# Chunk recurrence of an RWKV-7 mixer: two heads per full-array product, and the preparation of two pairs of heads side by side

## Chip, cores and metric

The kernel runs on one core of a Trainium2 chip, in one launch. The metric is the device time of that core in microseconds (us); lower is better. Several runs are timed and their median counts.

## What is computed

One residual block on x of 1024 frames x 1024 features: a SwiGLU layer, a mixer, a second SwiGLU layer, each behind an RMS norm whose shift, scale and gate come from a conditioning vector. Half of the mixer is chunked attention (8 heads of 64), half is the RWKV-7 recurrence (8 heads of 64), which is what the change touches:

```python
def step(state, inp):
    r_t, w_t, k_t, v_t, kk_t, b_t = inp
    sa = jnp.einsum('bhvk,bhk->bhv', state, -kk_t)
    state = (state * w_t[:, :, None, :] + sa[..., None] * b_t[:, :, None, :]
             + v_t[..., None] * k_t[:, :, None, :])
    y_t = jnp.einsum('bhvk,bhk->bhv', state, r_t)
    return state, y_t
...
_, ys = lax.scan(step, state0, seq_first)
```

Everything is computed in float32; the large products are split into three products of float32r parts.

## The kernel before

The 1024 frames are two halves, hf = 0 and 1, of 512 frames (8 chunks of 64). The order of all instructions is written at build time by a planner: tasks are Python generators that yield what they wait for, `drive` (L285) runs the one whose wait ends first on a modelled clock, and where nothing else is due it takes the next block of the **main products** (`mm`, tiles of 128x512 float32r, fed by weights that SyncE loads as `wst`, ScalarE rounds to `whi` and VectorE completes as `wlo`). So the products of attention and recurrence stand between main products on TensorE. The main products in their order are: first layer of half 0 (f1A), projection of half 0 (pA), first layer of half 1 (f1B), output projection of half 0 (oA), projection of half 1 (pB), second layer of half 0 (f2A), output projection of half 1 (oB), second layer of half 1 (f2B). Recurrence and attention of half 0 run beside f1B, those of half 1 beside f2A. Each engine executes its instructions in the planned order and waits for semaphores where data is late.

The recurrence works on four pairs of heads (p = 0 to 3) in each half, two pairs to a group:

- `rwkv1` (L1203) prepares one pair: masked products GR and GA (banks `gb`), transposed keys BKn (banks `bt`), decays `gC`. `RA` holds r and a, `BKB` the keys. In `rwkv` (L1542) the second pair's preparation starts when the first one's has ended.
- `inverse` (L1344) inverts the triangular 32x32 blocks of a group on VectorE, through DRAM (`nd`), and loads them into `TT`.
- `rwkv2` (L1386) is the recurrence of one pair. It completes `TT` by 32x32 products (`qb`, `ub`), then takes 8 chunks in turn. A chunk has three steps: `px` = GA·UV, copied to X; `pu` = TT·X, copied into UV; `pz` = BKn·UV, from which the next state Z and the next UV are made. Each step is one product per head, 64 columns wide: px and pz have 128 rows and 64 columns of the array (128*64), pu 64 and 64 (64*64), and the two heads take two tiles of the array. After the loop, `yb` reads all UV and Z at once. That is 3 steps x 8 chunks x 4 pairs x 2 halves = 192 steps.

UV is a tile of its own per head (16 loads `UV<-vs` of 128 KB each in all), filled with the values before `TT` is waited for. The pools `set0` and `set1` have 16 slots of 128x512 each.

Of the kernel before, what the change touches and what calls it, by code (L numbers as in the profile page):

```python
# [16 lines left out]
P = 128  # L17
# [228 lines left out]
class Builder:  # L246
# [113 lines left out]
    def setup(self):  # L360
# [3 lines left out]
        self.sets = [self.pool("set0", 16), self.pool("set1", 16)]  # L364
# [54 lines left out]
    def setup2(self):  # L419
# [107 lines left out]
    def ada_first(self, v):  # L527
# [5 lines left out]
        def load(i, v=v):  # L533
            q, kb = steps[i]
            n = 2 if (v, q) in ADA_PE else 2 if v or kb in (0, 3) else 3
            w[v, i] = self.tile(self.sets[1], "n1", 16, "wa", [P, 2, 256], reads=n)
            nc.sync.dma_start(w[v, i], self.a["w_ada"][v, :, 2 * kb : 2 * kb + 2, q * 256 : q * 256 + 256])
# [63 lines left out]
    def ada(self, vs):  # L601
# [101 lines left out]
    def norm_first(self):  # L703
# [18 lines left out]
        for q in range(4):  # L722
# [16 lines left out]
    def norm(self, key, hf, j, src=None):  # L739
        nc = self.nc  # L740
        s = self.sets[hf]
# [12 lines left out]
        nh, nl, vs = [], [], []  # L754
# [6 lines left out]
        def low(d):  # L761
            nc.vector.scalar_tensor_tensor(nl[d], vs[d], scale(d)[1], nh[d].bitcast(F32), op0=OP.add, op1=OP.subtract)

        def step(d, x):
            yield x, rstd, "th", f"n{hf}", lambda: 0.0 if len(self.mains) < 2 else self.clock.at["vector"]
            sc, sh = scale(d)
# [3 lines left out]
            nh.append(self.tile(s, f"n{hf}", 16, "nh", dt=F32R))  # L770
            nl.append(self.tile(s, f"n{hf}", 16, "nl", dt=F32R))
# [373 lines left out]
    def tb(self, hf, name, shape=None):  # L1145
        return self.tile(self.sets[hf], f"n{hf}", 16, name, shape)
# [56 lines left out]
    def rwkv1(self, hf, p):  # L1203
# [70 lines left out]
        BKB = self.sm("BKB", [P, NC, 3, C], 1)  # L1274
# [5 lines left out]
        nc.scalar.activation(BKB[:, :, 2], BKB[:, :, 0], AF.Copy)  # L1280
# [8 lines left out]
        GR, GA, BKn = [], [], []  # L1289
        for h in range(2):  # L1290
            yield f"n{hf}"
            GR.append(self.tb(hf, "GR", [P, NC, C]))
            yield f"n{hf}"
            GA.append(self.tb(hf, "GA", [P, NC, C]))
        half = [slice(0, 64), slice(64, 128)]
        for c4 in range(2):
            yield BKB, RA, self.two
            gb = [self.bank("gb", 2) for h in range(2)]
            for i in range(4):
                c = 4 * c4 + i  # L1300
                for h, s in enumerate(half):
                    self.mm(
                        gb[h][:, i * P : i * P + P],
                        BKB[s, c, h : h + 2].rearrange("p k t -> p (k t)"),
                        RA[s, c].rearrange("p k t -> p (k t)"), side=2,
                    )
            for h in range(2):
                g4 = gb[h].rearrange("p (c k t) -> p c k t", c=4, k=2)
                for k, o in ((1, GA[h]), (0, GR[h])):
# [7 lines left out]
        for c in range(NC):  # L1317
            for h, s in enumerate(half):
                self.tp_(
                    bt[h][:, c * C : c * C + C],  # L1320
                    BKB[s, c, h : h + 2].rearrange("p k t -> p (k t)"),
                    self.ident[s, s], side=2,
                )
        for h in range(2):
            yield f"n{hf}"
            BKn.append(self.tb(hf, "BKn", [P, NC, C]))
            nc.scalar.activation(BKn[h], c3(bt[h]), AF.Copy)
# [8 lines left out]
        for h in range(2):  # L1336
            yield GA[h]
            for b in range(2):
                q = h * 64 + b * 32
                w = (4 * i + 2 * h + b) * 8  # L1340
                nc.sync.dma_start(nd[w : w + 8].rearrange("c s t -> s c t"), GA[h][q : q + 32, :, b * 32 : b * 32 + 32])
        return dict(p=p, RA=RA, GR=GR, GA=GA, BKn=BKn, bon=bon, gC=gC)

    def inverse(self, hf, st):  # L1344
# [26 lines left out]
        for i in range(2):  # L1371
# [3 lines left out]
            nc.gpsimd.memset(TT, 0.0)  # L1375
        yield ud
        for i in range(2):
            for h in range(2):
                for b in range(2):
# [4 lines left out]
                    )  # L1384

    def rwkv2(self, hf, st):  # L1386
        nc = self.nc
        p, RA, GR, GA, BKn, TT = (st[k] for k in ("p", "RA", "GR", "GA", "BKn", "TT"))
# [12 lines left out]
        U1 = self.tr("U1", [P, NC, 32])  # L1401
        for h in range(2):
            r0 = slice(h * 64, h * 64 + 32)
            nc.vector.transpose(U1[r0], TT[r0, :, 0:32])
        yield U1, "b"
        qb = self.bank("qb", 2)
        for c in range(NC):
            for h in range(2):
                r0 = slice(h * 64, h * 64 + 32)
                r1 = slice(h * 64 + 32, h * 64 + 64)  # L1410
                self.mm(
                    qb[r1, c * 32 : c * 32 + 32], GA[h][r0, c, 32:64], U1[r0, c],
                    tile_position=(h * 64, h * 64 + 32), side=2,
                )
        yield qb
        for h in range(2):
            r1 = slice(h * 64 + 32, h * 64 + 64)
            nc.scalar.activation(U1[r1], qb[r1, 0:256].rearrange("p (c t) -> p c t", c=NC), AF.Copy)
        yield U1, TT, "b"
        ub = self.bank("ub", 2)  # L1420
        for c in range(NC):
            for h in range(2):
# [3 lines left out]
                    ub[r0, c * 32 : c * 32 + 32], U1[r1, c], TT[r1, c, 32:64],  # L1426
# [8 lines left out]
        nc.scalar.activation(GA[0][0:64], RA[0:64, :, 1], AF.Copy)  # L1435
        nc.gpsimd.tensor_copy(GA[1][64:128], RA[64:128, :, 1])

        Z = self.tr("Z", [P, NC, C])
        nc.vector.tensor_copy(Z[:, 0], self.Zc[p])
        for c in range(NC):  # L1440
            yield *GA, *UV, "b"
            px = self.bank("px")
            for h in range(2):
                self.mm(px[h * 64 : h * 64 + 64, 0:C], GA[h][:, c], UV[h][:, c], skip_group_check=True)
            X = self.sm("X", [P, C], 4, reads=2)
            nc.vector.tensor_copy(X, px[:, 0:C])
            zg = self.sm("zg", [P, C], 3, reads=3 if c + 1 < NC else 1)
# [276 lines left out]
```

## Time and profile before

| | us |
|---|---|
| median of 3 runs | 2178.19 (2175.65 to 2180.26) |
| profiled execution, time | 2181.82 |
| profiled execution, span of the trace | 2180.1 |
| PE (TensorE matmul) busy | 2136.9 |
| DVE (VectorE) busy | 1463.8 |
| ACT (ScalarE) busy | 897.1 |
| POOL (GpSimd) busy | 128.4 |

Engine shares are averages over stages with different limits. Matmul durations in the trace are modelled and overlap: what one costs is read from the distance between the starts of instructions. One product written in float32 is two instructions in the trace (so px counts 256 for 64 steps of two heads), one in float32r a single one. In the notation 128*64 128x64, the first pair is the rows and columns of the array in use, the second the partitions and elements that stream in. All 11568 matmul instructions of the program are in the trace.

### The profile page before, as it was taken

To read this page: it belongs to the slowest core of one execution; us is meant where nothing else is said; L and a number is where in the kernel's file an instruction comes from. 1 tells how busy PE (TensorE), PEld (TensorE's weight loads), DVE (VectorE), ACT (ScalarE), POOL (GpSimd) and SP (SyncE) were. 2 spreads that over 40 slices of the span, in tenths; PEclk is the share of its full clock that TensorE was granted. 3 is DMA by queue.
4 is the path that set the end of the run, shared out by engine and by line. 5 is a ranking of instruction groups with operands and counts; after the bars stand their busy time and mean duration, and the time that the engine had idled before them with its cause. 6 is when DMAs were issued, how large, how long until landed. Compare 5 with 4: busy or idle time off the path is not lost.

```text
span 2180.1 us, 32870 instructions
## 1 busy us (share of the span) xinstructions
PE 2136.9 (98%) x11568; PEld 1718.1 (79%) x11568; DVE 1463.8 (67%) x3090; ACT 897.1 (41%) x1712; POOL 128.4 (6%) x166
## 2 busy tenths in 40 slices
PE   6999999999999999999999999999999999999999
PEld 4788887888778868877888777867786888888887
DVE  6977777744578877877864567878787664444444
ACT  4332224445555344333555555435442343222322
POOL 1000000011300000000020300001000000000000
PEclk9999999999999999999999999999999999999999
DMA  7766655435764424334645745324432554433333
GB/s 236 243 201 210 202 161 173 132 116 160 234 189 132 121 71 125 105 94 123 215 153 163 217 146 159 110 81 128 120 106 64 184 167 141 136 97 98 96 93 102
DMA packets 230853, 316.31 MB, mean 145 GB/s; under 512 B 61976, under 2 KB 97824, under 8 KB 230688
## 3 DMA queue, kind: packets, MB, share of 16 engines
q1 hardware_dynamic: 230688, 314.22, 47.7%
q8 instruction: 91, 1.49, 0.3%
q14 instruction: 74, 0.61, 0.1%
HBM read 279.52 MB, written 34.61 MB: 144 GB/s over the span
## 4 chain that ended last, share of the span: by engine, by line
PE 86%; DMA 6%; DVE 4%; ACT 2%; issue 2%; SPq 1%; POOL 0%; DVEq 0%; ACTq 0%; POOLq 0%
PE mm L512 72%; PE mmb L512 3%; PE yp L512 1%; DMA vd<-av 1%; PE tr L516 1%; PE S L512 1%; DMA kd<-kT 1%; SPq L172 1%; PE cs L516 1%; DVE wlo L172 1%; PE gb L512 1%; PE pu L512 1%; DMA wst<-in_ffn_w 1%; PE px L512 1%; PE pz L512 1%
## 5 line engine op out<-in xcount | busy, mean ns | idle before, releaser
L172 ACT ACTIVATE whi<-wst 128x512 fp32r<-128x512 f32 (+2 forms) x692 | 423.2, 613 | 840.2 <-PE mm L512 692.1
L172 DVE TENSOR_TENSOR wlo<-wst,whi 128x512 fp32r<-128x512 f32 (+2 forms) x692 | 462.3, 671 | 341.2 <-ACT whi L172 328.0
L512 PE MATMUL mm<-nh,whi 128*128 128x512 f32 x1520 | 616.7, 406 | 0.0
L512 PE MATMUL mm<-nl,whi 128*128 128x512 f32 x1520 | 594.2, 391 | 4.3 <-DVE nl L172 4.3
L512 PE MATMUL mm<-nh,wlo 128*128 128x512 f32 x1520 | 594.8, 391 | 0.0
L512 PEld LDWEIGHTS mm<-nh,wlo 128*128 128x128 f32 x1520 | 286.0, 188 | 61.4
L512 PEld LDWEIGHTS mm<-nh,whi 128*128 128x128 f32 x1520 | 286.7, 189 | 56.4 <-issue 1.9
L512 PEld LDWEIGHTS mm<-nl,whi 128*128 128x128 f32 x1520 | 286.8, 189 | 56.1 <-DVE nl L172 5.7
L512 PE MATMUL mm<-ah,whi 128*128 128x512 f32 x670 | 273.3, 408 | 2.1 <-ACT ah L172 1.2
L512 PE MATMUL mm<-al,whi 128*128 128x512 f32 x670 | 262.4, 392 | 1.5 <-DVE al L172 1.5
L512 PE MATMUL mm<-ah,wlo 128*128 128x512 f32 x670 | 262.5, 392 | 1.1 <-DVE wlo L172 1.1
L172 DVE SCALAR_TENSOR_TENSOR h<-mm,g,h 128x512 f32<-128x512 f32 x183 | 135.9, 746 | 89.6 <-PE mm L512 88.9
L512 PEld LDWEIGHTS mm<-ah,whi 128*128 128x128 f32 x670 | 126.5, 189 | 30.1 <-ACT ah L172 2.1
L512 PEld LDWEIGHTS mm<-ah,wlo 128*128 128x128 f32 x670 | 126.3, 188 | 28.6 <-DVE wlo L172 1.5
L512 PEld LDWEIGHTS mm<-al,whi 128*128 128x128 f32 x670 | 126.6, 189 | 24.8 <-DVE al L172 2.4
L172 ACT ACTIVATE E<-E,st 128x640 f32<-128x640 f32 (+4 forms) x128 | 85.8, 688 | 32.4 <-DVE st L172 32.0
L172 DVE SCALAR_TENSOR_TENSOR acc<-wa,silc,acc 128x512 f32<-128x512 f32 (+1 forms) x120 | 83.5, 705 | 0.6
L172 DVE TENSOR_TENSOR sw<-sw,mm 128x512 f32<-128x512 f32 x85 | 58.4, 687 | 35.7 <-PE mm L512 32.3
L172 ACT ACTIVATE pt<-tr 128x256 fp32r<-128x256 f32 x144 | 49.4, 344 | 65.8 <-PE tr L516 60.4
L512 PE MATMUL mm<-whi,nh 128*128 128x512 f32 x184 | 73.8, 401 | 0.0
L512 PE MATMUL mm<-wlo,nh 128*128 128x512 f32 x184 | 71.8, 390 | 0.0
L512 PE MATMUL mm<-whi,nl 128*128 128x512 f32 x184 | 71.7, 390 | 0.0
(247 smaller groups left out, 2631.3 us busy)
## 6 DMA issues: line engine op xcount, KB each, us to landing
wst<-in_ffn_w SPq DMA_DIRECT2D x468, 256.0 KB, 2.8
wa<-in_w_ada SPq DMA_DIRECT2D x144, 256.0 KB, 4.0
wst<-in_w_v SPq DMA_DIRECT2D x64, 256.0 KB, 2.9
wst<-in_ffn_w SPq DMA_DIRECT2D x64, 192.0 KB, 2.4
wst<-in_w_t SPq DMA_DIRECT2D x40, 256.0 KB, 4.1
wst<-in_w_out SPq DMA_DIRECT2D x32, 256.0 KB, 3.0
kd<-kT SPq DMA_DIRECT2D x48, 128.0 KB, 3.9
bias<-in_bias SPq DMA_DIRECT2D x16, 320.0 KB, 4.2
```

What stands on the lines that cost most here:

```text
L172: return f(*args, **kw)
L512: self.nc.tensor.matmul(out, lhsT, rhs, start=start, stop=stop, **kw)
L516: self.nc.tensor.transpose(out, in_, ident)
```

## The change

- The three steps of a chunk become one product each of 128 rows and 128 columns, with the two heads side by side in the streamed 128 columns or, in pu, on the diagonal of a 128x128 tile X (`Xd`, cleared once). pu takes two neighbouring chunks of TT as its 128 columns and uses 64 of the rows that come out.
- GA, BKn and UV hold both heads in one tile. UV is now a part of RA (its second and third column blocks), so the mask part of RA is first copied to GA, by ScalarE for both heads; the values are loaded after that, in one load of 256 KB per pair.
- X is copied half by VectorE, half by ScalarE; UV is copied by ScalarE for both heads; Z is copied from UV by ScalarE, where VectorE computed it a second time.
- TT's first blocks of the second head are loaded once more to partitions 0 to 31 (`T1`), and both heads' `qb` products read rows 0 to 31 of the array.
- The preparations of the two pairs of a group are tasks of their own: the second starts when RA of the first is written (`RA` in `done`), and in the second group each follows the recurrence of a pair of the first.
- The pools `set0` and `set1` become 8 slots of 128x512 and 4 of twice that; the ring `tr` has 8 slots for 10. The low parts `nl`, `ml` and some weights `wa` go in twos into the large slots. `mx` moves from the ring `th` to `tr`.

The core of the diff:

```diff
-        self.sets = [self.pool("set0", 16), self.pool("set1", 16)]
+        self.sets = [self.pool("set0", 8), self.pool("set1", 8)]
...
+        self.Xd = [cp.tile([P, P], F32, name=f"Xd{i}") for i in range(4)]
+        for x in self.Xd:
+            nc.gpsimd.memset(x, 0.0)
...
+    def slot(self, hf, name, shape=None, dt=F32, reads=None):
+        return self.tile(self.sets[hf], f"n{hf}", 8, name, shape, dt, reads)
+    def slots(self, hf, name, shape, dt=F32, reads=None):
+        return self.tile(self.sets[hf], f"d{hf}", 4, name, shape, dt, reads)
...
-        return self.tile(self.sp, "tr", 10, name, shape, dt, reads)
+        return self.tile(self.sp, "tr", 8, name, shape, dt, reads)
...
-        RA = self.sm("RA", [P, NC, 2, C], 2)
+        RA = self.sm("RA", [P, NC, 3, C], 2)
...
+        self.done.add(f"RA{hf}{p}")
...
-        nc.scalar.activation(BKB[:, :, 2], BKB[:, :, 0], AF.Copy)
...
+        yield f"d{hf}"
+        GA = self.slots(hf, "GA", [P, NC, 2, C])
...
+            yield "tr"
+            st[i]["T1"] = self.tr("T1", [32, NC, 32], reads=1)
...
-        UV = []
-        vsr = self.vs[hf].rearrange("(c t) f -> t c f", t=C)
-        for h in range(2):
-            yield "tr"
-            UV.append(self.tr("UV", [P, NC, C]))
-            o = slice(64 - h * 64, 128 - h * 64)
-            nc.vector.tensor_copy(UV[h][h * 64 : h * 64 + 64, 0], self.Zc[p][h * 64 : h * 64 + 64])
-            nc.sync.dma_start(UV[h][o], vsr[:, :, p * P + h * C : p * P + h * C + C])
-        yield TT, "tr"
-        U1 = self.tr("U1", [P, NC, 32])
-        for h in range(2):
-            r0 = slice(h * 64, h * 64 + 32)
-            nc.vector.transpose(U1[r0], TT[r0, :, 0:32])
+        heads = [slice(0, 64), slice(64, 128)]
+        hv = lambda t: t.rearrange("p h v -> p (h v)")
+        yield TT, T1, "tr"
+        U1 = self.tr("U1", [P, 2, NC, 32])
+        nc.vector.transpose(U1[0:32, 0], TT[0:32, :, 0:32])
+        nc.vector.transpose(U1[0:32, 1], T1)
...
-                    qb[r1, c * 32 : c * 32 + 32], GA[h][r0, c, 32:64], U1[r0, c],
-                    tile_position=(h * 64, h * 64 + 32), side=2,
+                    qb[r1, c * 32 : c * 32 + 32], GA[0:32, c, h, 32:64], U1[0:32, h, c],
+                    tile_position=(0, h * 64 + 32), side=2,
...
-        nc.scalar.activation(GA[0][0:64], RA[0:64, :, 1], AF.Copy)
-        nc.gpsimd.tensor_copy(GA[1][64:128], RA[64:128, :, 1])
+        for h, s in enumerate(heads):
+            nc.scalar.activation(GA[0:64, :, h], RA[s, :, 1], AF.Copy)
+        yield GA
+        UV = RA[:, :, 1:3]
+        for h, s in enumerate(heads):
+            nc.vector.tensor_copy(UV[0:64, 0, h], self.Zc[p][s])
+        vsr = self.vs[hf].rearrange("(c t) f -> t c f", t=C)
+        nc.sync.dma_start(
+            UV[64:128].rearrange("p c h v -> p c (h v)"), vsr[:, :, cs]
+        )
         Z = self.tr("Z", [P, NC, C])
         nc.vector.tensor_copy(Z[:, 0], self.Zc[p])
+        Tf = TT.rearrange("p c t -> p (c t)")
         for c in range(NC):
-            yield *GA, *UV, "b"
-            px = self.bank("px")
-            for h in range(2):
-                self.mm(px[h * 64 : h * 64 + 64, 0:C], GA[h][:, c], UV[h][:, c], skip_group_check=True)
-            X = self.sm("X", [P, C], 4, reads=2)
-            nc.vector.tensor_copy(X, px[:, 0:C])
-            zg = self.sm("zg", [P, C], 3, reads=3 if c + 1 < NC else 1)
+            yield GA, UV, "b"
+            px = self.bank("px", 2)
+            self.mm(px[:, 0:P], hv(GA[:, c]), hv(UV[:, c]))
+            X = self.Xd[p % 2 * 2 + c % 2]
+            nc.vector.tensor_copy(X[0:64, 0:64], px[0:64, 0:64])
+            nc.scalar.activation(X[64:128, 64:128], px[64:128, 64:128], AF.Copy)
+            zg = self.sm("zg", [P, C], 3, reads=2)
             gc = st["gC"][:, c : c + 1]
             nc.vector.tensor_scalar(zg, Z[:, c], gc, None, OP.mult)
             yield X, TT, "b"
-            pu = self.bank("pu", 2)[:, 0:C]
-            for h in range(2):
-                s = slice(h * 64, h * 64 + 64)
-                self.mm(pu[s], TT[s, c], X[s])
-            nc.scalar.activation(UV[0][0:64, c], pu[0:64], AF.Copy)
-            nc.vector.tensor_copy(UV[1][64:128, c], pu[64:128])
-            yield *UV, "b"
-            pz = self.bank("pz", 3 if c + 1 < NC else 1)[:, 0:C]
-            for h in range(2):
-                s = slice(h * 64, h * 64 + 64)
-                self.mm(pz[s], BKn[h][:, c], UV[h][:, c])
-            for h in range(2 if c + 1 < NC else 0):
-                s = slice(h * 64, h * 64 + 64)
-                nc.vector.scalar_tensor_tensor(UV[h][s, c + 1], pz[s], gc[s], zg[s], op0=OP.mult, op1=OP.add)
-            zn = Z[:, c + 1] if c + 1 < NC else self.Zc[p]
-            nc.vector.scalar_tensor_tensor(zn, pz, gc, zg, op0=OP.mult, op1=OP.add)
-        self.free(TT, *BKn)
+            pu = self.bank("pu", 1)
+            t = min(c, NC - 2) * C
+            self.mm(pu[:, 0:P], Tf[:, t : t + P], X)
+            nc.scalar.activation(hv(UV[0:64, c]), pu[heads[c == NC - 1], 0:P], AF.Copy)
+            yield BKn, UV, "b"
+            pz = self.bank("pz", 2)
+            self.mm(pz[:, 0:P], hv(BKn[:, c]), hv(UV[:, c]))
+            for h, s in enumerate(heads):
+                zn = UV[0:64, c + 1, h] if c + 1 < NC else self.Zc[p][s]
+                nc.vector.scalar_tensor_tensor(zn, pz[s, h * 64 : h * 64 + 64], gc[s], zg[s], op0=OP.mult, op1=OP.add)
+            for h, s in enumerate(heads if c + 1 < NC else []):
+                nc.scalar.activation(Z[s, c + 1], UV[0:64, c + 1, h], AF.Copy)
+        self.free(TT, BKn)
...
-    def rwkv(self, hf, g, st):
-        if g == 0:
-            yield from self.rwkv_prep(hf)
-        for i in range(2):
-            st.append((yield from self.rwkv1(hf, 2 * g + i)))
-        yield from self.inverse(hf, st)
     def spawn_rwkv(self, name, hf, after):
-        v = f"{name}v"
+        v, up = f"{name}v", f"{name}p"
         self.spawn(v, self.values(hf), 3, [f"v{hf}"])
+        self.spawn(up, self.rwkv_prep(hf), 2, after)
+        before = [up, up]
         for g in range(2):
-            st = []
-            self.spawn(f"{name}{g}", self.rwkv(hf, g, st), 2, after)
-            after = []
+            st = {}
+            pre = [f"{name}{g}p{i}" for i in range(2)]
+            for i in range(2):
+                x = [before[i]] + [f"RA{hf}{2 * g}"] * i
+                self.spawn(pre[i], self.late(lambda st=st, p=2 * g + i: self.rwkv1(hf, p, st)), 2, x)
+            self.spawn(f"{name}{g}", self.late(lambda st=st: self.inverse(hf, st)), 2, pre)
+            before = []
             for i in range(2):
                 n = f"{name}{g}_{i}"
                 self.spawn(n, self.late(lambda st=st, i=i: self.rwkv2(hf, st[i])), 2 + i, [f"{name}{g}", v])
-                after.append(n)
-        self.spawn(name, self.end_rwkv(), 2, after)
+                before.append(n)
+        self.spawn(name, self.end_rwkv(), 2, before)
```

On TensorE, in the recurrence of the first two pairs of half 0, before (`yp` is a product of attention, `nh`, `nl` are the parts of the normed input):

```order
L512 MATMUL px_7680<-UV_7434,GA_6332 64x64
L512 MATMUL px_7680<-UV_7437,GA_6334 64x64
L512 MATMUL mm_7592<-nh_3569,whi_7451 128x512
L512 MATMUL mm_7592<-nl_3570,whi_7451 128x512
L512 MATMUL mm_7592<-nh_3569,wlo_7452 128x512
L512 MATMUL pu_7695<-X_7683,TT_7396 64x64 x2
L512 MATMUL pu_7700<-X_7668,TT_7398 64x64 x2
L512 MATMUL yp_7705<-pt_7634,V_7216 128x256 x2
L516 MATMUL tr_7708<-ident,E_7477 128x128
L516 MATMUL tr_7708<-ident,E_7507 128x128
```

and in the changed kernel (UV bears the name of its tile, RA; X that of its tile, Xd):

```order
L523 MATMUL pu_7622<-Xd_2991,TT_7279 128x128
L523 MATMUL pu_7626<-Xd_2990,TT_7276 128x128
L523 MATMUL mm_7561<-nh_3535,whi_7421 128x512
L523 MATMUL mm_7561<-nl_3491,whi_7421 128x512
L523 MATMUL mm_7561<-nh_3535,wlo_7422 128x512
L523 MATMUL pz_7634<-RA_6225,BKn_6474 128x128
L523 MATMUL pz_7640<-RA_6496,BKn_6694 128x128
L523 MATMUL mm_7561<-nh_3550,whi_7421 128x512
L523 MATMUL mm_7561<-nl_3547,whi_7421 128x512
L523 MATMUL mm_7561<-nh_3550,wlo_7422 128x512
L523 MATMUL px_7652<-RA_6225,GA_6349 128x128
```

Two products of 64x64 (two rows, or one with x2) have become one of 128x128. Main products stand between the steps as before.

On SyncE, where the recurrence of the first group begins, before (`nd_1` is the inverse on its way back, `vs` holds the values):

```order
L172 DMA nd_1_3089<-BKB_6866 64x1024
L172 DMA wst_7415<-in_ffn_w 128x512
L172 DMA TT_7396<-nd_1_3089 32x8x32 x4
L172 DMA TT_7398<-nd_1_3089 32x8x32 x4
L172 DMA UV_7434<-vs_3080 64x8x64
L172 DMA UV_7437<-vs_3080 64x8x64
L172 DMA UV_7440<-vs_3080 64x8x64
L172 DMA UV_7443<-vs_3080 64x8x64
L172 DMA wst_7455<-in_ffn_w 128x512
```

and in the changed kernel:

```order
L172 DMA TT_7276<-nd_1_3030 32x8x32 x4
L172 DMA T_1675_7278<-nd_1_3030 32x8x32
L172 DMA TT_7279<-nd_1_3030 32x8x32 x4
L172 DMA T_1677_7281<-nd_1_3030 32x8x32
L172 DMA wst_7323<-in_ffn_w 128x512
L172 DMA wst_7342<-in_ffn_w 128x512
L172 DMA wst_7369<-in_ffn_w 128x512
L172 DMA wst_7463<-in_ffn_w 128x512
L172 DMA RA_6225<-vs_3021 64x8x128
L172 DMA kd_7523<-kT_3025 64x512 x2
L172 DMA qd_7526<-qT_3023 64x512 x2
L172 DMA RA_6496<-vs_3021 64x8x128
```

The values go to RA instead of UV, in one load per pair instead of two, and behind four loads of weights where they stood right behind those of TT.

## Rows read from the trace of the kernel before

**Rows 1.** Page, part 1: busy us, share of the span, instructions.

```profile
PE 2136.9 (98%) x11568; PEld 1718.1 (79%) x11568; DVE 1463.8 (67%) x3090; ACT 897.1 (41%) x1712; POOL 128.4 (6%) x166
```

**Rows 2.** Page, part 4: the chain that ended last, by engine.

```profile
PE 86%; DMA 6%; DVE 4%; ACT 2%; issue 2%; SPq 1%; POOL 0%; DVEq 0%; ACTq 0%; POOLq 0%
```

**Rows 3.** PE timeline at 763 us: start, duration, instruction; one step between main products.

```profile
762.94 0.39 PE L512 MATMUL mm<-nl,whi 128*128 128x512 f32 x1
763.17 0.40 PE L512 MATMUL mm<-nh,wlo 128*128 128x512 f32 x1
763.49 0.34 PE L512 MATMUL px<-UV,GA 128*64 128x64 f32 x4
...
764.09 0.39 PE L512 MATMUL mm<-nl,whi 128*128 128x512 f32 x1
```

**Rows 4.** PE timeline at 803 us: two steps of one tiling.

```profile
802.93 0.39 PE L512 MATMUL mm<-nh,wlo 128*128 128x512 f32 x1
803.25 0.34 PE L512 MATMUL pz<-UV,BKn 128*64 128x64 f32 x4
803.41 0.29 PE L512 MATMUL px<-UV,GA 128*64 128x64 f32 x4
...
803.97 0.39 PE L512 MATMUL mm<-nl,whi 128*128 128x512 f32 x1
```

**Rows 5.** PE timeline at 974 us: two steps of different tilings.

```profile
974.08 0.39 PE L512 MATMUL mm<-ah,wlo 128*128 128x512 f32 x1
974.40 0.33 PE L512 MATMUL pu<-X,TT 64*64 64x64 f32 x4
974.66 0.34 PE L512 MATMUL px<-UV,GA 128*64 128x64 f32 x4
...
975.26 0.39 PE L512 MATMUL mm<-al,whi 128*128 128x512 f32 x1
```

**Rows 6.** PE timeline at 1010 us: four full-array float32 products of 128 columns.

```profile
1010.61 0.39 PE L512 MATMUL mm<-nh,wlo 128*128 128x512 f32 x1
1010.84 1.05 PE L512 MATMUL gate<-wu,sgd 128*128 128x128 f32 x8
...
1011.96 0.40 PE L512 MATMUL mm<-nl,whi 128*128 128x512 f32 x1
```

**Rows 7.** Groups by form: instructions, count, busy us, mean ns, idle before.

```profile
L512 PE MATMUL px<-UV,GA 128*64 128x64 f32 x256 | 21.3, 242 | 0.2 <-DVE Z L172 0.2
```

**Rows 8.** The same groups: the 32x32 products that complete TT.

```profile
L512 PE MATMUL qb<-U,GA 32*32 32x32 f32 x256 | 5.5, 192 | 0.0
```

**Rows 9.** ACT groups at the start of a recurrence.

```profile
L172 ACT ACTIVATE TT<-ub 32x256 f32<-32x256 f32 x16 | 6.0, 372 | 3.3 <-PE ub L512 3.2
L172 ACT ACTIVATE GA<-RA 64x512 f32<-64x512 f32 x8 | 5.1, 633 | 0.2
```

**Rows 10.** DMA issues: count, KB each, median us from issue to landing.

```profile
UV<-vs SPq DMA_DIRECT2D x16, 128.0 KB, 3.1
vn<-vs SPq DMA_DIRECT2D x8, 256.0 KB, 4.7
```

**Rows 11.** VectorE and ScalarE groups of a chunk.

```profile
L172 DVE COPY UV<-pu 64x64 f32<-64x64 f32 x64 | 14.1, 227 | 19.9 <-ACT UV L172 18.5
L172 DVE SCALAR_TENSOR_TENSOR Z<-pz,gC,zg 128x64 f32<-128x64 f32 x56 | 15.9, 284 | 1.6
L172 ACT ACTIVATE UV<-pu 64x64 f32<-64x64 f32 x64 | 13.5, 217 | 88.6 <-PE pu L512 81.2 <-DVE D L172 5.3 <-DVE zg L172 1.6
```

**Rows 12.** Windows, 500 to 1700 us: busy us of PE, PEld, DVE, ACT, POOL.

```profile
500.00:1700.00 1200.00, 1183.28 (x7324) 937.84 (x7323) 875.20 (x2130) 553.50 (x1130) 103.57 (x131) 1.00 0.46 137
```

**Rows 13.** SP timeline at 1012 us: five weight loads issued.

```profile
1012.24 10.52 SPq L172 DMA_DIRECT2D wst<-in_ffn_w  x5
```

**Rows 14.** Waits of PE: us in total, times, longest us.

```profile
PE row L512 <- DMA wa<-in_w_ada: 12.2, 1, 12.2
PE mm L512 <- DVE nl L172: 4.3, 2, 3.3
```

More of the change, by code (lines that the diff above doesn't have):

```diff
@@ L535, in load @@
             n = 2 if (v, q) in ADA_PE else 2 if v or kb in (0, 3) else 3
-            w[v, i] = self.tile(self.sets[1], "n1", 16, "wa", [P, 2, 256], reads=n)
+            if v == 0:
+                w[v, i] = self.slot(1, "wa", [P, 2, 256], reads=n)
+            else:
+                if i % 2 == 0:
+                    w["two"] = self.slots(1, "wa", [P, 2, 2, 256], F32, reads=2 * n)
+                w[v, i] = w["two"][:, i % 2]
             nc.sync.dma_start(w[v, i], self.a["w_ada"][v, :, 2 * kb : 2 * kb + 2, q * 256 : q * 256 + 256])
@@ L732, in norm_first @@
             for d in two:
-                yield t[d % 2], "n0"
-                nl.append(self.tile(self.sets[0], "n0", 16, "nl", dt=F32R))
-                nc.vector.scalar_tensor_tensor(nl[d], xr[d], scale(d), t[d % 2], op0=OP.mult, op1=OP.subtract)
+                if d % 2 == 0:
+                    yield t[d % 2], "d0"
+                    lows = self.slots(0, "nl", [P, 2, H], F32R)
+                yield t[d % 2]
+                nc.vector.scalar_tensor_tensor(lows[:, d % 2], xr[d], scale(d), t[d % 2], op0=OP.mult, op1=OP.subtract)
+                nl.append(lows[:, d % 2])
                 if d == 0:
@@ L1272, in rwkv1 @@
         self.free(gp)
+        self.done.add(f"RA{hf}{p}")
         yield RA, "BKB"
-        BKB = self.sm("BKB", [P, NC, 3, C], 1)
+        BKB = self.sm("BKB", [P, NC, 2, C], 1)
         nc.vector.scalar_tensor_tensor(rn, rn, 0.5, gi, op0=OP.mult, op1=OP.mult)
@@ L1287, in rwkv1 @@
         self.free(rs)
-        GR, GA, BKn = [], [], []
+        GR = []
         for h in range(2):
@@ L1303, in rwkv1 @@
                         gb[h][:, i * P : i * P + P],
-                        BKB[s, c, h : h + 2].rearrange("p k t -> p (k t)"),
-                        RA[s, c].rearrange("p k t -> p (k t)"), side=2,
+                        BKB[s, c].rearrange("p k t -> p (k t)"),
+                        RA[s, c, 0:2].rearrange("p k t -> p (k t)"), side=2,
                     )
@@ L1308, in rwkv1 @@
                 g4 = gb[h].rearrange("p (c k t) -> p c k t", c=4, k=2)
-                for k, o in ((1, GA[h]), (0, GR[h])):
+                for k, o in ((1, GA[:, :, h]), (0, GR[h])):
                     nc.vector.tensor_mul(
@@ L1320, in rwkv1 @@
                     bt[h][:, c * C : c * C + C],
-                    BKB[s, c, h : h + 2].rearrange("p k t -> p (k t)"),
+                    BKB[s, c].rearrange("p k t -> p (k t)"),
                     self.ident[s, s], side=2,
                 )
+        yield f"d{hf}"
+        BKn = self.slots(hf, "BKn", [P, NC, 2, C])
         for h in range(2):
-            yield f"n{hf}"
-            BKn.append(self.tb(hf, "BKn", [P, NC, C]))
-            nc.scalar.activation(BKn[h], c3(bt[h]), AF.Copy)
+            yield bt[h]
+            nc.scalar.activation(BKn[:, :, h], c3(bt[h]), AF.Copy)
         self.free(BKB)
@@ L1473, in rwkv2 @@
         sm = self.sm("sm", [P, 4, 4, 2], 2)
-        yield Z, *UV, self.two
+        yield Z, UV, self.two
         yb = [self.bank("yb", 2) for h in range(2)]
@@ L1480, in rwkv2 @@
             for c in range(NC):
-                self.mm(out(h, c), GR[h][:, c], UV[h][:, c], start=c < 2, stop=False, skip_group_check=True)
+                self.mm(out(h, c), GR[h][:, c], UV[:, c, h], start=c < 2, stop=False, skip_group_check=True)
         for c in range(NC):
@@ L1586, in mixed @@
             if c < 8:
-                yield "th"
-                q.append(self.th("mx", 2))
+                yield "tr"
+                q.append(self.tr("mx", reads=2))
                 nc.sync.dma_start(q[-1], self.mix[hf][c])
@@ L1592, in mixed @@
             m = q.popleft()
-            yield m, f"n{hf}"
-            hi = self.tile(self.sets[hf], f"n{hf}", 16, "mh", dt=F32R)
-            lo = self.tile(self.sets[hf], f"n{hf}", 16, "ml", dt=F32R)
+            yield m, f"n{hf}", *([] if len(nh) % 2 else [f"d{hf}"])
+            hi = self.slot(hf, "mh", dt=F32R)
+            if len(nh) % 2 == 0:
+                two = self.slots(hf, "ml", [P, 2, H], F32R)
+            lo = two[:, len(nh) % 2]
             nc.scalar.activation(hi, m, AF.Copy)
             nh.append(hi)
-            nl.append(lo)
             yield hi
             nc.vector.tensor_sub(lo, m, hi.bitcast(F32))
+            nl.append(lo)
     def wout(self, key, hf):
```

42 lines of the change are left out of this document (22 added, 20 removed).

## Prediction, before the changed kernel ran

> **What bounds the kernel.** I read the page's busy shares first: PE is busy 2136.9 us of 2180.1, the next engine 67% [rows 1]. The chain that ended last agrees: 86% of it is PE [rows 2]. "Busy" overlaps, so the second look is whether PE waits or works where the recurrence runs: between 500 and 1700 us it is idle for 1200 - 1183.28 = 16.7 us only, at the full granted clock of 1.00, that is 2.4 GHz [rows 12]. So main products fill every gap of the recurrence, and the length of its chain of copies and products is not what counts. What counts is how much of TensorE's time each step takes from the main products. That is read from starts in the timeline, not from durations.
>
> Main products start 0.23 us apart. Around one px step, from the main product before it to the second one behind it, 0.92 us pass (763.17 to 764.09), where two starts alone would take 0.46: the step costs **0.46 us** [rows 3]. Two steps of the same tiling side by side cost 803.97 - 802.93 - 0.46 = **0.58 us** together [rows 4], two of different tilings 975.26 - 974.08 - 0.46 = **0.72 us** [rows 5]. So a second step in the same tiling adds 0.12 us, and entering and leaving a tiling about 0.34 us. The full array with float32 shows in `gate`: four products of 128 columns between main products take 1011.96 - 1010.61 - 0.46 = 0.89 us, **0.22 us each** [rows 6].
>
> **The 192 steps, before and after.** px, pu and pz have 256 instructions each [rows 7], two per product and two products per step: 64 steps each, 192 in all. In the order of the kernel before I count the neighbours: 67 steps stand alone between full-array work, 62 stand as 31 twos of one tiling, 52 as 26 twos of different tilings, 11 in longer tiled runs with yb or ub. Cost: 67 x 0.46 = 30.8, 31 x 0.58 = 18.0, 26 x 0.72 = 18.7, 11 x 0.12 = 1.3, together 68.8 us. Afterwards all 192 are full-array products between full-array products: 192 x 0.22 = 42.2 us, so **-26 us** on PE. The order confirms the cause: changes of the tiling from one product to the next fall from 390 to 111, while the number of main products stays. Bounds: -31 if the 11 steps cost 0.46 as well and twos were dearer elsewhere, -20 if a lone full-array product costs 0.25, since rows 6 show four in a run.
>
> **Weighed against a rule.** By rows 4 the two heads in two tiles cost 0.12 us where the array is already tiled, against 0.22 for the full array. The Trainium skill, page TensorEngine Tiling (Array Packing), section Overview, says that the full array is underused at contractions or widths of 64 and that tiles there give up to twice the speed, which speaks against this change. By that alone the 192 steps would get dearer by 192 x 0.10 = 19 us; by rows 3 the change of tiling outweighs it, because a step here seldom has a tiled neighbour.
>
> **Other products.** In qb both heads now read the same 32 rows. If the pairs no longer overlap, the 5.5 us of qb [rows 8] double; if the columns alone keep them apart, nothing. I take +1 (range 0 to 5.5), as px with both heads on the same rows does overlap (0.12 us per step). ub, qb and yb lose some tiled neighbours: four more entries, 4 x 0.34 = +1.
>
> **The values' load.** Before, UV was loaded ahead of TT's completion and cost nothing. Now it waits for the GA copies. In the order, from the last ub product of the first pair to its first px stand 20 full-width products (4.6 us), a qb and an ub of 5.5 / 8 = 0.7 each and two shorter ones: 6.0 to 6.4 us of cover. In it must go two TT copies (2 x 0.37) and two GA copies (2 x 0.63) on ScalarE [rows 9], 2.0 us, and the load of 256 KB, which lies between the 3.1 us of the old 128 KB loads and the 4.7 of another 256 KB load from the same tensor [rows 10]: 5.1 to 6.7 us. PE, which runs in order, waits 0 to 0.7 us at each of the 8 recurrences; I take 0.25, **+2 us** (0 to 5.6). T1's eight small loads run with those of TT and are covered by the same products.
>
> **VectorE and ScalarE.** Per chunk VectorE loses a copy of UV (0.227) and the second computation of Z (0.284): 64 x 0.51 = 33 us less. ScalarE takes over half of X, a wider copy of UV and two copies of Z; with 0.217 per small copy [rows 11] some 0.7 us per chunk, 45 us more, less one BKB copy per pair. Both are hidden by main products: VectorE was busy 875 and ScalarE 553 of 1200 us [rows 12]. If that cover went, ScalarE's copies would stand behind whi conversions (second rival). GpSimd only loses GA copies. Pools and rings hold the same bytes; nl and ml in twos move no work.
>
> **The overlapped preparation** moves products, not their number, and PE is filled, so by itself it gives nothing. It ends the recurrences of half 0 sooner, and what PE idles from 500 to 1700 us (16.7) can shrink or grow with the new plan: I take -2 (-8 to +10). The opening, where PE waits 12.2 us for the first weights and 4.3 for nl [rows 14], is also planned anew: 0, plus or minus 4.
>
> **Sum:** -26 + 1 + 1 + 2 - 2 = -24 us against the profiled execution (2181.8, span 2180.1). The median of the runs, 2178.2, lies 3.6 us under it; the same difference gives **2154 us**. A change within 0.2% (4.4 us) can't be told from none here.
>
> **Rivals.**
> 1. *The values' load becomes the wait: slower.* On SyncE it stands behind four weight loads, and where their slots are taken these leave only every 10.52 / 5 = 2.1 us [rows 13]. If the queue is two slots behind plan when a recurrence begins, each of the 8 waits 4.2 + 0.7 us: +39, less 26, +13: 2191 us. It decides from 26 / 8 = 3.2 us per recurrence. Against it: the weight loads before were in the same queue in front of TT's loads and PE was idle 16.7 us in all.
> 2. *ScalarE makes the chunks late.* X is complete when the later of two engines has copied it, and another copy of 512 columns can stand in front (0.63 us, [rows 9]). If that costs PE 0.2 us at each of 64 chunks, 13 us go: 2167 us. For it: every chunk now needs ScalarE twice more. Against it: so far ScalarE waits for PE in front of its UV copies (81.2 us), and not PE for ScalarE [rows 11].
> 3. *The full array is dearer than two tiles:* the 0.34 us would be no price of the tiling but of any interruption, and a lone full-array product would pay it too, on top of the 0.10 it is dearer. Then 192 x 0.10 = +19 and +2 of the other terms: 2199 us. Against it: gate interrupts as well and pays nothing of the kind.
> 4. *The freed time is lost to waits of the new plan* (idle time grows from 17 to some 40 us, as VectorE is denser in the overlapped preparation): 2178 us.
>
> **How the numbers follow.** Forecast 0.78, rivals 0.06, 0.10, 0.02, 0.04. The forecast's own range comes from its bounds, which will not all fall on one side: about 2140 to 2170. With the second rival inside, 2138 to 2172 holds 8 in 10. Under 2173.8 lie the forecast, but for 0.01, and most of rival 2 (0.09): faster 0.86. Within 0.2%: rival 4 and the edges, 0.06. Slower: rivals 1 and 3, 0.08.
>
> **What would show it.** Right: px, pu and pz with 128 instructions each; a lone step costs 0.22 us between main products; main products start 0.23 us apart on both sides of it; PE idle between 500 us and the end of the second recurrence stays near 17 us; the first px of a recurrence waits under 1 us for the load. Wrong: lone steps above 0.3 us; PE waits on UV's load or on X of several us; VectorE idle less than before in spite of less work.

## The result, and the profile after

The changed kernel takes **2151.65 us** (median of 4 runs, 2149.62 to 2152.22) against 2179.23 us of the kernel before (2175.65 to 2183.69): ratio 0.9871, 95% interval 0.9851 to 0.9891. It is faster by 27.6 us. The forecast was 2154 us. One of the six runs of px_pz_tiled below had a granted clock of 0.655 and took 2997.76 us; its median is that of the other five, and its trace is not read.

The page's busy row and the chain that ended last, for [rows 1, 2]:

```profile
PE 2112.8 (98%) x11184; PEld 1733.7 (81%) x11184; DVE 1442.2 (67%) x2978; ACT 942.1 (44%) x1888; POOL 125.4 (6%) x162
...
PE 87%; DMA 4%; DVE 3%; ACT 2%; issue 2%; SPq 1%; POOL 0%; DVEq 0%; ACTq 0%; POOLq 0%
```

The profiled span fell from 2180.1 to 2150.2 us. PE's busy time gives 2136.9 - 2112.8 = 24.1 of these 29.9 us, its idle time (43.2 to 37.4) the other 5.8. PE still bounds the kernel.

The PE timeline, for [rows 3 to 5]: start, duration, instruction. First a lone step, then two steps together.

```profile
804.26 0.39 PE L523 MATMUL mm<-nh,wlo 128*128 128x512 f32 x1
804.49 0.38 PE L523 MATMUL pu<-Xd,TT 128*128 128x128 f32 x2
804.63 0.47 PE L523 MATMUL mm<-nh,whi 128*128 128x512 f32 x1
804.95 0.39 PE L523 MATMUL mm<-nl,whi 128*128 128x512 f32 x1
...
778.83 0.40 PE L523 MATMUL mm<-nh,wlo 128*128 128x512 f32 x1
779.06 0.38 PE L523 MATMUL pz<-RA,BKn 128*128 128x128 f32 x2
779.28 0.39 PE L523 MATMUL pu<-Xd,TT 128*128 128x128 f32 x2
779.43 0.47 PE L523 MATMUL mm<-nh,whi 128*128 128x512 f32 x1
779.74 0.39 PE L523 MATMUL mm<-nl,whi 128*128 128x512 f32 x1
```

By the measure of the prediction a lone step costs 804.95 - 804.26 - 0.46 = **0.23 us** (0.46 before), two together 779.74 - 778.83 - 0.46 = **0.45 us** (0.58 or 0.72 before). That is the 0.22 us of `gate` [rows 6]: these steps pay nothing for entering a tiling. Not every step is as cheap. Over the whole trace, 47 steps of the change stand alone with main products on both sides; idle time taken off, their median is 0.23 us and their mean 0.27, because 11 of the 24 px among them cost 0.27 to 0.47. Why these do is not shown. Before, 41 such steps have a median of 0.47 and a mean of 0.48 us.

The groups of the steps on PE, with `qb`, for [rows 7, 8]: count, busy us, mean ns, idle before.

```profile
L523 PE MATMUL px<-RA,GA 128*128 128x128 f32 x128 | 26.8, 293 | 1.2 <-DMA RA<-vs 0.8 <-DVE RA L172 0.2
L523 PE MATMUL pu<-Xd,TT 128*128 128x128 f32 x128 | 24.1, 282 | 0.6 <-ACT Xd L172 0.6
L523 PE MATMUL pz<-RA,BKn 128*128 128x128 f32 x128 | 23.9, 277 | 0.0
...
L523 PE MATMUL qb<-U,GA 32*32 32x32 f32 x256 | 5.5, 192 | 0.0
```

Busy time per product went up (px 21.3 to 26.8 us) while the steps became cheaper: the starts of the neighbours tell the cost, the durations do not. `qb` is as long as before, although both heads now read the same rows.

The copies of a chunk, DVE and ACT groups, for [rows 9, 11]. Of the kernel before, two that the rows do not have, then of the change:

```profile
L172 DVE SCALAR_TENSOR_TENSOR UV<-pz,gC,zg 64x64 f32<-64x64 f32 x112 | 31.6, 282 | 10.7 <-PE pz L512 8.4
L172 DVE COPY X<-px 128x64 f32<-128x64 f32 x64 | 14.0, 219 | 13.3 <-PE px L512 12.8
```

```profile
L172 DVE SCALAR_TENSOR_TENSOR RA<-pz,gC,zg 64x64 f32<-64x64 f32 x112 | 31.6, 282 | 20.5 <-PE pz L523 18.1
L172 DVE TENSOR_SCALAR zg<-Z,gC 128x64 f32<-128x64 f32 x64 | 15.6, 243 | 0.7
L172 DVE COPY Xd<-px 64x64 f32<-64x64 f32 x64 | 13.7, 214 | 10.7 <-PE px L523 9.3
...
L172 ACT ACTIVATE Z<-RA 64x64 f32<-64x64 f32 x112 | 28.6, 255 | 32.0 <-DVE RA L172 28.0
L172 ACT ACTIVATE RA<-pu 64x128 f32<-64x128 f32 x64 | 16.6, 268 | 9.9 <-PE pu L523 8.8
L172 ACT ACTIVATE Xd<-px 64x64 f32<-64x64 f32 x64 | 13.8, 218 | 25.9 <-DVE Xd L172 24.8
L172 ACT ACTIVATE GA<-RA 64x512 f32<-64x512 f32 x16 | 10.1, 632 | 0.3
```

The window of 500 to 1700 us, for [rows 12], and the waits of PE, for [rows 14] (us in total, times, longest):

```profile
500.00:1700.00 1200.00, 1188.35 (x7075) 978.07 (x7074) 876.63 (x2053) 612.18 (x1331) 102.35 (x124) 1.00 0.48 143
```

```profile
PE row L523 <- DMA wa<-in_w_ada: 13.5, 1, 13.5
...
PE px L523 <- DMA RA<-vs: 0.8, 3, 0.4
...
PE pu L523 <- ACT Xd L172: 0.6, 2, 0.3
...
PE mm L523 <- DVE nl L172: 0.4, 1, 0.4
```

In the window PE is idle 11.65 us for 16.7. The values' load makes PE wait 0.8 us in all, ScalarE's copies of X 0.6 us.

### The profile page after: what moved, and what is told of

Its sections match the earlier page's. It is cut to its first block, busy times and chain, and to the rows that moved or that the text cites. A ratio compares the mean times of both kernels' runs of the same rounds, so it can differ in the third digit from the quotient of the medians.

```text
span 2150.2 us, 32194 instructions
## 1 busy us (share of the span) xinstructions
PE 2112.8 (98%) x11184; PEld 1733.7 (81%) x11184; DVE 1442.2 (67%) x2978; ACT 942.1 (44%) x1888; POOL 125.4 (6%) x162
## 4 chain that ended last, share of the span: by engine, by line
PE 87%; DMA 4%; DVE 3%; ACT 2%; issue 2%; SPq 1%; POOL 0%; DVEq 0%; ACTq 0%; POOLq 0%
PE mm L523 73%; PE mmb L523 3%; PE yp L523 1%; PE S L523 1%; SPq L172 1%; PE tr L527 1%; PE px L523 1%; PE cs L527 1%; PE gb L523 1%; DVE wlo L172 1%; PE pu L523 1%; DMA kd<-kT 1%; PE pz L523 1%; DMA wst<-in_w_t 1%; DMA vd<-av 1%
## 5 line engine op out<-in xcount | busy, mean ns | idle before, releaser
L172 ACT ACTIVATE pt<-tr 128x256 fp32r<-128x256 f32 x144 | 49.1, 346 | 51.2 <-PE tr L527 46.8
```

The lines of the kernel that those rows point to most:

```text
L172: return f(*args, **kw)
```

## The experiments

Three parts of the change can be had apart: the **products** (full array, both heads side by side, with their layout and all that the other two leave: the pools, the load of the values, the copies of GA), the **overlap** of the preparations, and the **relief** (some 24 us of small copies that go from VectorE to ScalarE). In this table idle is the profile's span less PE's busy time, and VectorE the busy time of its row on the page.

| products | overlap | relief | median us | PE busy | PE idle | VectorE | kernel |
|---|---|---|---|---|---|---|---|
| no | no | no | 2179 | 2136.9 | 43.2 | 1463.8 | before |
| no | yes | no | 2170.63 | 2132.7 | 35.9 | 1466.3 | overlap_only |
| no | no | yes | 2174.21 | 2133.0 | 38.1 | 1440.3 | relief_only |
| no | yes | yes | 2174.36 | 2134.6 | 40.8 | 1442.4 | overlap_relief |
| no | yes | yes, other order | 2182.74 | 2134.2 | 44.7 | 1440.3 | or_replan |
| yes | no | yes | 2167.33 | 2120.1 | 44.7 | 1441.0 | products_only |
| yes | yes | mostly no | 2160.13 | 2117.7 | 41.1 | 1457.2 | z_back |
| yes | yes | yes | 2151.65 | 2112.8 | 37.4 | 1442.2 | the change |
| yes | yes | yes, other order | 2153.93 | 2111.8 | 35.3 | 1439.0 | after_replan |

### The overlap alone, and the products without it

overlap_only is the kernel before with the tasks of the change; products_only is the changed kernel with the second preparation behind the first:

```diff
-                x = [before[i]] + [f"RA{hf}{2 * g}"] * i
+                x = [[*before, pre[0]][-1]] if i else list(before)
```

> The kernel before with the overlapped preparation alone; the recurrence keeps two tiled products per step. Theory (the changes of tiling around the steps are what was saved): the planned order still has 392 changes of tiling (390 before), and by the prices of the prediction the steps cost 67.8 us for 68.8, so 2178 us, within 4 of the kernel before. Rival (the overlap ends the recurrences sooner and so saves waits): at least 8 us of the gain come from here, 2170 us or less.

Measured: 2170.63 us, ratio 0.9963 (0.9951 to 0.9975).

> The changed kernel with the preparations of a group one after the other again, as before. Theory: 114 changes of tiling (111), same number of main products: 2152 us, within 4 of the changed kernel. Rival (overlap): 2160 us or more.

Measured: 2167.33 us, ratio 0.9953 (0.9936 to 0.997). Without the overlap 15.7 of the 27.6 us are gone (17.9, plus or minus 6, by the ratios). One place shows where. products_only, waits of PE from 1000 to 1060 us, then two windows (us, PE busy, PEld, DVE, ACT, POOL, granted clock, DMA share, GB/s):

```profile
PE cs L527 <- DVE ssq L172: 2.8, 1, 2.8
PE mm L523 <- ACT mh L172: 1.5, 1, 1.5
PE mm L523 <- DVE ml L172: 0.9, 3, 0.3
```

```profile
1030.00:1042.00 12.00, 9.28 (x41) 7.34 (x40) 12.00 (x21) 8.04 (x14) 0.00 (x0) 1.00 1.02 363
1042.00:1056.00 14.00, 11.49 (x33) 7.65 (x34) 11.33 (x19) 7.33 (x12) 1.01 (x1) 0.64 0.48 171
```

The changed kernel, the same windows:

```profile
1030.00:1042.00 12.00, 12.00 (x55) 9.89 (x54) 11.18 (x20) 7.16 (x12) 0.00 (x0) 1.00 0.95 306
1042.00:1056.00 14.00, 14.00 (x70) 11.77 (x69) 11.77 (x19) 7.32 (x12) 1.01 (x1) 1.00 0.61 197
```

This is where TensorE goes from f1B to the output projection of half 0 (oA), whose inputs `mh` and `ml` are made from `mx`, the mixer's result read back. VectorE is full (12.00 of 12 us), PE waits 5.2 us, and then its granted clock falls to 0.64 of 2.4 GHz in the mean, so part of the stretch ran at 1.2. Products of oA there last up to 0.80 us instead of 0.39 (PE timeline of products_only, first the longest wait):

```profile
1042.11 0.82 PE L527 MATMUL cs<-ident,ssq 128*128 128x128 f32 x4 [2.83 <-DVE ssq L172]
...
1052.14 0.80 PE L523 MATMUL mm<-ml,whi 128*128 128x512 f32 x1 [0.28 <-DVE ml L172]
1052.73 0.63 PE L523 MATMUL mm<-mh,wlo 128*128 128x512 f32 x1
```

The longest wait is for `ssq`, a sum for a norm, not for `mh`. In the changed kernel `cs` starts at nearly the same time, without a wait, because 15 products of oA stand before it:

```profile
1041.90 0.60 PE L527 MATMUL cs<-ident,ssq 128*128 128x128 f32 x4
```

In products_only only six stand there. What the stretch costs shows in the main products (`mm` and `mmb`), 7896 in either kernel: the 3750th starts at 1046.7 us in the change and at 1056.9 in products_only. So some 10 of the 14.6 us between the two spans are lost by then, about as much as 5.2 us of waits and 14 x (1 - 0.64) = 5.0 us for the lower clock make. The other 4.4 are lost later, and their cause stays open. The cause of the 10 shows in the first loads of `mx` and the first oA products (per tile: durations min/median/max, first and last start). Of the kernel before, of products_only and of the change:

```profile
L172 SPq DMA_DIRECT2D mx<-mix x16: 319/404/448, 1023.3 to 1709.6; - x16
...
L512 PE MATMUL mm<-mh,whi x128: 389/389/478, 1047.3 to 1766.1; 128*128 128x512 f32 x128
```

```profile
L172 SPq DMA_DIRECT2D mx<-mix x16: 378/420/822, 1029.1 to 1707.2; - x16
...
L523 PE MATMUL mm<-mh,whi x128: 388/389/796, 1037.8 to 1750.8; 128*128 128x512 f32 x128
```

```profile
L172 SPq DMA_DIRECT2D mx<-mix x16: 377/424/1103, 1001.9 to 1686.4; - x16
...
L523 PE MATMUL mm<-mh,whi x128: 389/389/478, 1038.5 to 1736.1; 128*128 128x512 f32 x128
```

From the first `mx` to the first product of oA the kernel before had 24.0 us. With cheaper steps f1B is through some 9 us sooner (1047.3 to 1037.8), and without the overlap the recurrence of half 0 also ends 5.8 us later than before (1023.3 to 1029.1; why, these rows do not show): 8.7 us are left, and PE waits. With the overlap 36.6 us are left, and it does not. Most of the recurrence's cover had gone, and the overlap put it back. products_only was not written in a second order.

The kernel before has a smaller wait in this stretch, 1.5 us for f1B's own inputs, and a lower clock with it:

```profile
1030.00:1042.00 12.00, 10.47 (x38) 7.95 (x38) 11.44 (x20) 8.11 (x16) 0.00 (x0) 0.86 0.76 236
```

### The price of a step, by undoing and by doubling

pz_tiled is the changed kernel with pz in two tiles again; px_pz_tiled does the same for px; px_twice issues every full-array px product twice.

```diff
-            self.mm(pz[:, 0:P], hv(BKn[:, c]), hv(UV[:, c]))
+            for h, s in enumerate(heads):
+                self.mm(pz[s, h * 64 : h * 64 + 64], BKn[:, c, h], UV[:, c, h], skip_group_check=True)
```

> The changed kernel, but pz is again two products in two tiles of 128*64, on the same data; X, UV, copies and everything else stay. Theory: changes of tiling rise from 111 to 205; 37 lone steps at 0.46 us, 9 twos at 0.58 and 9 beside other tiled work at 0.12 make 23.3 us where 64 full-array steps at 0.22 make 14.1: 9 us more, 2161 us. Rival (the full array is dearer than two tiles): 64 x 0.10 = 6 us less, 2146 us. Rival (the gain came from the copies, the layout or the overlap): no change, 2152 us.

Measured: 2155.79 us, ratio 0.9898 (0.9879 to 0.9916).

> As pz_tiled, with px in two tiles as well. Theory: 304 changes of tiling; 72 lone steps at 0.46, 24 twos at 0.58 and 8 beside other tiled work make 48.0 us for 28.2: 20 us more, 2172 us, about twice the step of pz_tiled. Rival (full array dearer): 13 us less, 2139 us. Rival (copies, layout, overlap): 2152 us.

Measured: 2163.68 us, ratio 0.9936 (0.992 to 0.9953).

> The changed kernel with each px product issued twice in a row into the same bank, the second overwriting the first: 64 more full-array products, nothing else. Theory (TensorE has no slack, and a full-array step costs 0.22 us of its time): 64 x 0.22 = 14 us more, 2166 us. Rival (the chain of copies bounds the recurrence and TensorE has slack there): 2152 to 2155 us.

Measured: 2167.0 us, ratio 0.9952 (0.9936 to 0.9967).

64 more full-array products cost 15.4 us of time, 0.24 each, and 2125.5 - 2112.8 = 12.7 us of PE's busy time, 0.20 each: the 0.22 of the prediction lies between. (Beside px_twice and vector_back the kernel before took 2176.83 us, 2.4 less than above; by the ratios px_twice costs 17.6 us, plus or minus 6.) The tiles cost 4.1 and 12.0 us where 9 and 20 were expected: the sign and the growth are right, the size is about half. pu, the third kind of step, was not put back into tiles, so undoing shows 12.0 of the 22.7 us that the products bring (next but one section); what pu and the new layout bring was not measured apart. The price itself is back in pz_tiled, in its PE timeline: 764.06 - 763.13 - 0.46 = 0.47 us for a lone pz.

```profile
763.13 0.40 PE L523 MATMUL mm<-nh,wlo 128*128 128x512 f32 x1
763.46 0.34 PE L523 MATMUL pz<-RA,BKn 128*64 128x64 f32 x4
763.73 0.50 PE L523 MATMUL mm<-nh,whi 128*128 128x512 f32 x1
764.06 0.40 PE L523 MATMUL mm<-nl,whi 128*128 128x512 f32 x1
```

### Is VectorE covered?

vector_back is the changed kernel with the second half of X, the copy of UV and the copies of Z on VectorE; z_back moves the copies of Z alone; zg_scalar goes the other way and gives ScalarE one VectorE instruction per chunk.

```diff
-            nc.scalar.activation(X[64:128, 64:128], px[64:128, 64:128], AF.Copy)
+            nc.vector.tensor_copy(X[64:128, 64:128], px[64:128, 64:128])
...
-            nc.scalar.activation(hv(UV[0:64, c]), pu[heads[c == NC - 1], 0:P], AF.Copy)
+            nc.vector.tensor_copy(hv(UV[0:64, c]), pu[heads[c == NC - 1], 0:P])
...
-                nc.scalar.activation(Z[s, c + 1], UV[0:64, c + 1, h], AF.Copy)
+                nc.vector.tensor_copy(Z[s, c + 1], UV[0:64, c + 1, h])
```

> The changed kernel with the second half of X, the copy of UV and the copies of Z on VectorE instead of ScalarE: about 0.7 us of VectorE per chunk, some 45 us more of its time, more than the change took from it. The products stay. Theory (the engines' copies are covered by main products): 2152 to 2156 us. Rival (a good part of the gain is the relief of VectorE, which is busy 73% from 500 to 1700 us): 10 us more or worse, 2162 us or above.

Measured: 2174.76 us, ratio 0.999 (0.998 to 1.0). 49.8 us more on VectorE take back 23.1 of the 27.6 us (25.9, plus or minus 5, by the ratios). vector_back, busy row, waits of PE, and windows:

```profile
PE 2122.7 (98%) x11184; PEld 1731.8 (80%) x11184; DVE 1492.0 (69%) x3218; ACT 889.4 (41%) x1648; POOL 126.2 (6%) x162
```

```profile
PE gb L523 <- DVE BKB L172: 3.7, 1, 3.7
...
PE pu L523 <- DVE Xd L172: 3.6, 9, 0.5
...
PE px L523 <- DVE RA L172: 2.1, 7, 0.4
```

```profile
700.00:1000.00 300.00, 296.27 (x1939) 237.85 (x1938) 252.93 (x684) 110.05 (x211) 14.07 (x21) 1.00 0.36 103
1500.00:1700.00 200.00, 193.20 (x1263) 158.50 (x1262) 170.20 (x461) 86.63 (x167) 9.64 (x13) 0.99 0.34 98
```

The changed kernel, the same windows:

```profile
700.00:1000.00 300.00, 298.33 (x2010) 246.09 (x2009) 238.48 (x584) 141.12 (x338) 18.48 (x24) 1.00 0.37 107
1500.00:1700.00 200.00, 198.86 (x1260) 164.30 (x1259) 159.44 (x400) 104.72 (x237) 7.22 (x11) 1.00 0.41 119
```

Where the recurrences run VectorE is at 84 and 85%, and now makes PE wait for X, for RA (the next Z) and for the keys BKB. PE's idle time grows by 49.1 - 37.4 = 11.7 us; its busy time grows by 9.9 us too, which these rows do not explain. Whether VectorE's load counts here, or that the two halves of X now follow one another on one engine and make each chunk longer, these runs do not part.

> The changed kernel with the copies that form Z written by VectorE again: some 21 to 24 us more of VectorE, the same less of ScalarE. Theory (0.46 us per us of VectorE): about 2152 + 10 = 2162 us. Rival (VectorE is covered): 2152 to 2155 us.

Measured: 2160.13 us, ratio 0.9916 (0.99 to 0.9932): 8.5 us for 15.0 us more on VectorE.

```diff
-            nc.vector.tensor_scalar(zg, Z[:, c], gc, None, OP.mult)
+            nc.scalar.activation(zg, Z[:, c], AF.Copy, scale=gc)
```

> The changed kernel with the scaling of the gate's result (64 instructions, 15.6 us of VectorE) done by ScalarE instead. Theory (0.46 us per us of VectorE): about 2152 - 7 = 2145 us. Rival (VectorE is covered, or ScalarE becomes late): 2152 us or more.

Measured: 2156.47 us, ratio 0.9901 (0.9883 to 0.9919). 10.5 us less on VectorE and 20.2 more on ScalarE make it 4.8 us slower, not 7 faster. So VectorE's work is not worth a fixed sum per microsecond. That less of it gives nothing is not shown, since ScalarE had more to do here.

### Relief and overlap without the products

relief_only is the kernel before with the copies of UV and Z where the change has them:

```diff
-            nc.vector.tensor_copy(UV[1][64:128, c], pu[64:128])
+            nc.scalar.activation(UV[1][64:128, c], pu[64:128], AF.Copy)
...
-            nc.vector.scalar_tensor_tensor(zn, pz, gc, zg, op0=OP.mult, op1=OP.add)
+            if c + 1 < NC:
+                for h in range(2):
+                    s = slice(h * 64, h * 64 + 64)
+                    nc.scalar.activation(Z[s, c + 1], UV[h][s, c + 1], AF.Copy)
```

> The kernel before, with the second head's copy of UV and the Z that is formed from UV written by ScalarE instead of VectorE: some 30 us of VectorE's 1463.8 move to ScalarE; the products stay in tiles and the preparations stay one after the other. Theory (VectorE's work counts, at about the 23/50 = 0.46 us per us that the run with work given back to VectorE showed): about 2179 - 14 = 2165 us. Rival, the prediction's own step (VectorE is covered): 2178 us, within 0.2% of before.

Measured: 2174.21 us, ratio 0.9983 (0.9973 to 0.9994): 4.4 us, neither theory's number.

> The kernel before with the overlapped preparation and the same relief of VectorE, that is nearly all of the change but the full-array products. Theory (the lone steps' price, some 23 us, comes on top of the other two): about 2175 us, as little as overlap and relief then leave. Rival (overlap and relief each bring what they bring alone, 8 and up to 14 us, and the full-array products only the rest): 2157 to 2165 us.

Measured: 2174.36 us, ratio 0.9985 (0.9973 to 0.9997). The theory holds: overlap and relief together bring some 4 us, and the products the other 22.7.

### How much is the luck of one order

Each of these edits also makes the planner write another order. Two runs change nothing but that:

```diff
-    SEM = 0.21
+    SEM = 0.19
```

> The changed kernel, instruction for instruction the same work, but written in another order: the planner's modelled delay from one engine to the next is 0.19 us for 0.21. Theory (the products bring their 23 us on top of overlap and relief; another order shifts the time by a few us only): 2152 plus or minus 5 us. Rival (2151.65 is the luck of one order): 2160 us or more, where the versions with small edits, 2156 to 2160, would be the rule.

Measured: 2153.93 us, ratio 0.989 (0.9873 to 0.9908).

> The kernel before with overlap and relief (2174.36 us), the same work in another order, by the same edit of the planner. Theory (without the full-array products no order of it comes near the change): 2174 plus or minus 5 us, some 20 us over the changed kernel in its own other order. Rival (2174.36 is an unlucky order, since the overlap alone took 2170.63): 2164 us or less, which would leave the products 12 us at most.

Measured: 2182.74 us, ratio 1.0016 (1.0005 to 1.0028).

The changed kernel moves by 2.3 us, the one with overlap and relief by 8.4 us, more than was expected. In this order the products are worth 28.8 us. By the ratios the products' part is 24.8 us in the first order and 27.4 in the second, each plus or minus 5. A single difference of up to 8 us (overlap_only, relief_only, pz_tiled, zg_scalar) can be one order's luck, and z_back's 8.5 is at that edge; those of 12 us and more (px_pz_tiled, px_twice, products_only, vector_back) lie beyond it, but each was seen in one order only, and two second orders are few to draw the edge from. No version was faster than the change.

## Why the prediction was right, and which steps failed

The total was right within 2.4 us, and its largest term in kind and nearly in size. That the total came so near is in part luck: without the overlap, which the prediction counted at nothing, the same products end at 2167.33 us, 13 us over the forecast.

- **The steps, -26 us: holds, given the rest.** A lone step fell from 0.46 to 0.23 us in the median, though to 0.27 in the mean, and PE's busy time fell by 24.1 us. By the means of the steps that stand between main products, alone or in groups, the 192 take some 72 us before and 50 after, an estimate: 22 us, between the 26 and its bound of 20; on top of overlap and relief the products brought 22.7 and 28.8 us in two orders. Without the overlap they brought 2174.21 - 2167.33 = 6.9 us.
- **"By itself it gives nothing" (the overlapped preparation): the number could stand, the reasoning failed.** Alone it brought 8.0 us, which an order's luck can be; beside relief nothing (2174.21 and 2174.36). But the prediction read PE's fill in the kernel before and took it to hold afterwards. Faster steps bring oA forward by 9 us, and the recurrence of half 0 would have come late: in this change the overlap holds 15.7 us, by one order. The rival that was missing is exactly this: the freed time is lost where half 0 is handed over.
- **"Both are hidden by main products" (VectorE's 33 us, ScalarE's 45): failed for VectorE.** Its mean of 875 of 1200 us [rows 12] hid that it is at 80% where the recurrences run (238.48 of 300 us from 700 us on in the change, 239.28 before), and putting 49.8 us on it cost 23.1. What taking work off it brings alone stays open: 4.4 us in relief_only, within one order's luck. The size was off too: VectorE lost 21.6 us, not 33. The copies of UV (14.1 us) and the 56 second computations of Z (15.9) did go, [rows 11]; but the last state of each recurrence is not computed twice, as the 64 of the sum had it, and is now written in two halves of 64 partitions that each take as long as one of 128 (16 at 283 ns for 8 at 280, 2.3 us more). The remaining 6 us were not traced; `D<-D,sm` alone took 4.2 us longer. ScalarE gained 45.0 us: the 45 of the chunks, with the second head's GA copy (5.0) in the place of the BKB copy (4.9).
- **qb, +1: 0.** The group kept its 5.5 us; two heads on the same rows and different columns still overlap.
- **The values' load, +2: 0.8 us** over all recurrences; the cover of 6.0 to 6.4 us was enough.
- **The opening, 0 plus or minus 4:** the waits for `wa` grew by 1.3 us, those for `nl` fell by 3.9 [rows 14], and the 250th main product starts 1.1 us later than before.

Of the rivals, the first (the load, from 26 us of waits on) found 0.8 us, the second (ScalarE late, 13 us) 0.6 us, and the fourth (lost to the new plan) saw idle time fall. The third, dearer products, needed a lone full-array step to pay for the interruption, 0.34 us on top of 0.22; it cost 0.23. The Trainium skill's rule (page TensorEngine Tiling (Array Packing), section Overview), that tiles are the faster way at widths of 64, did not decide: 0.47 us for a lone tiled pz and 0.23 for a lone full-array step speak against it where single steps stand between full-array products.

## What to carry to other kernels

Price a small product by the starts of its neighbours, at the place where it stands: here half-filled full-array products were cheaper than tiles where they stood alone between full-array work (0.23 against 0.46 us). Where one engine is full and a chain beside it just fits, making that engine faster moves the chain's deadline forward: look for the hand-over, and count what shortens the chain as part of the gain. Before believing a few microseconds of one edit to a planned kernel, write the same work in a second order; here that alone moved the time by 2 to 8 us.

## What was not expected of the hardware

- One wait of 2.8 us and a few shorter ones were followed by a granted clock of 0.64 in the next 14 us (products_only, 1042 to 1056 us), with main products of 0.63 to 0.80 us instead of 0.39. In the kernel before, waits of 1.5 us in all were followed by main products of 0.63 us too, with a granted clock of 0.86 from 1030 to 1042 us. So a wait on PE can cost more than its own length.
- 64x64 and 128x64 results cost VectorE the same: 282 and 284 ns for the scaled sums, 214 and 219 ns for the copies of X.
- The same instructions in another order differ by 8.4 us of 2174 (overlap_relief and or_replan). The two profiled executions differ by 3.5 us, with PE's busy time the same (2134.6 and 2134.2 us) and 3.9 us more of idle time.
